# A hybrid DeltaNet and mLSTM trunk: the scheduler plays the program on its detailed machine model

## The chip, the cores and the metric

The kernel runs on one NeuronCore of a Trainium2 chip. The metric is the device time of one execution in microseconds (us). Five engines work side by side, each through its own fixed list of instructions: TensorE (PE; its weight loads are shown apart as PEld), VectorE (DVE), ScalarE (ACT), GpSimd (POOL) and SyncE (SP), which here only issues transfers. An engine goes through its list in order; an instruction whose input is not there yet holds up what stands behind it.

## What is computed

The reference is a trunk of two layers over 1040 tokens (16 learned ones and 1024 from the input) of width 1024. Each layer is a mixer and then a feed-forward block (FFN) with a causal convolution, each between two RMS norms. The first mixer is a gated DeltaNet with 16 value heads, the second an mLSTM with 4 heads. Cut to its core:

```python
for i in range(DEPTH):                      # DEPTH = 2
    a_in = rms_norm(hs, norm_w[i, 0])
    mix = gated_deltanet(a_in, ...) if i % 2 == 0 else mlstm(a_in, ...)
    hs = hs + keep * rms_norm(mix, norm_w[i, 1])
    f = conv_ffn(rms_norm(hs, norm_w[i, 2]), ...)
    hs = hs + keep * rms_norm(f, norm_w[i, 3])

# gated_deltanet, per head and chunk
a_mat = eye + einsum('id,jd->ij', kb, kc) * decay * strict
sol = triangular_solve(a_mat, rhs, lower=True)
v_new = u_c - w_c @ S
o_c = qd_c @ S + att_c @ v_new
S = S * gt_c + kt_c.T @ v_new

# conv_ffn
u = causal_depthwise_conv(h @ w_up, conv_w) + conv_b
return (silu(gate) * up) @ w_down
```

## The kernel before

Activations lie with the features on the 128 partitions and the tokens along the free axis. The DeltaNet and the mLSTM work on three blocks of 348 tokens, each of three chunks of 116; the FFN works on two halves of 520 tokens, each of two quarters of 260.

**Products.** A float32 product is made of three matmuls on split operands, high by high, high by low and low by high (`mm3`, lines 233 to 235). A weight is loaded raw by SyncE, its high part is made by ScalarE and its low part by GpSimd (`split_slot`):

```python
nc.scalar.copy(hi, part(raw))                                             # L137
nc.gpsimd.tensor_tensor(lo, part(raw), hi.bitcast(F32), ALU.subtract)     # L138
```

There are 9 slots for raw weights and 10 for split ones. A load into a raw slot waits until GpSimd has read the slot.

**Stages.** First the DeltaNet. Its work is cut into 24 steps, one for each pair of value heads and each block. In a step the function `weave` interleaves, in the program's text, the preparation of the next step (`gdn_prepare`), the recurrence of this one (`gdn_recur`), the finish of the last one and a share of the input projection (`gdn_project`, tiles named `pj_gi`). Near the end of the stage a first part of the output projection (`dn_go`) takes the place of the input projection. Then come the rest of the output projection with its norms, the FFN with its up projection (`up`; seven products per weight block in place of eight, whose partial sums VectorE adds at line 196) and its down projection (`dn_f`), the mLSTM, and the second FFN.

**The triangular inverse.** For each head `inverse` builds a masked matrix, starts the inverse from its 2 x 2 blocks and doubles the block size six times. VectorE writes the first `Z` at line 920, and three matmuls read it at once:

```python
nc.vector.tensor_tensor(Z, l0, Ib, ALU.add)                               # L920
px = bank("px", 0)
for c in range(NC_B):
    nc.tensor.matmul(px[:, c * CH : (c + 1) * CH], Z[:, c, :], I, ...)    # L923
nc.scalar.copy(f2(X), px[:, :BS])                                         # L924
```

Ahead of it VectorE makes `ah` (line 911) and `l0`. Each of the six levels then has three visits to TensorE (lines 949, 958 and 963) with a VectorE or ScalarE operation behind each; two more visits (lines 969 and 977) end it, and line 979 writes the result `XT`. Line 750 writes the normalised key at the beginning of `gdn_prepare`.

**The norms.** Squares are made by ScalarE (line 294) and added by VectorE (line 295); one matmul with a matrix of ones sums them over the partitions (line 302), and the call around it asks that it stay behind the matmul before it in the program:

```python
self.tc.keep_in_program_order(nc.tensor.matmul(ps, self.ones_f32, acc, ...))   # L302
```

The residual stream is updated at lines 352 and 353.

**What sets the order.** The kernel's text names the engine of every instruction, but it does not write the engines' lists. When the `TileContext` of line 1484 closes, a scheduler plays the whole program on a model of the machine. Whenever an engine of the model can take an instruction, it gets the one that is earliest in the program among those whose inputs and whose buffer slot are there in the model at that moment; a block under `high_priority(n)` counts as so many places earlier. The order in which the model took the instructions is the list of each engine on the chip, and the slot that a tile got there is its slot. The waits are put in afterwards. So a duration in the model moves an instruction in the list, and nothing moves any more once the program is compiled.

Of the kernel before, what the change touches and what calls it, by code (L numbers as in the profile page):

```python
# [1476 lines left out]
def build(nc, arrays):  # L1477
    from contextlib import ExitStack

    a = {}  # L1480
    for n, v in arrays.items():
        a[n] = nc.dram_tensor(f"in_{n}_dram", v.shape, mybir.dt.from_np(v.dtype), kind="ExternalInput").ap()
    a["out"] = nc.dram_tensor("out_0_dram", (D, SEQ), F32, kind="ExternalOutput").ap()
    with tile.TileContext(nc) as tc, ExitStack() as ctx:  # L1484
        Trunk(tc, a).run(ctx)


# [10 lines left out]
```

## Time and profile before

| quantity | value |
|---|---|
| runs shown, median (lowest to highest) | 3448.46 us (3437.92 to 3455.48), 3 runs |
| the profiled execution | 3444.23 us |
| its span, first to last instruction | 3442.5 us |
| mean granted TensorE clock | 0.969 |
| loaded and stored | 297.75 MB, 86 GB/s over the span |
| transfer engines busy, main queue | 26.3% |

Busy time and span are of the one profiled execution. A matmul's row lasts longer than the time until the next one can start, since matmuls overlap; so a busy TensorE is not TensorE at its peak, and the idle time, with what ended it, is what a change of order can act on. The stages by their lines: the DeltaNet runs until about 1160 us, its output projection until about 1300, the first FFN's up projection from about 1380 to 1830 and its down projection to about 2130, the mLSTM to about 2580, and the second FFN to the end.

### The profile page before, as it was taken

The page shows a single profiled execution, that of the slowest core. Times are in us where ns is not written, and L with a number is a line of the kernel's source. Part 1 is how long each engine was busy: PE and PEld are TensorE (multiplying, and loading weights), DVE is VectorE, ACT ScalarE, POOL GpSimd, SP SyncE. Part 2 cuts the span into 40 slices and gives each one's busy share as a digit, 9 for nine tenths or more (in the row PEclk, how much of TensorE's full clock was granted, in tenths as well). Part 3 has the DMA queues.
Part 4 walks back from the last instruction along what each step waited for, and adds up shares of the span by engine and source line. Part 5 has one row for each costly group of instructions (what it writes and reads, how often), then busy time and mean ns, then how long its engine had stood idle before and what let it go on. Part 6 is the DMA issues. An engine that isn't in the chain of part 4 may idle for free. (4 is left out here: it accounts for less than half of the span.)

```text
span 3442.5 us, 68429 instructions
## 1 busy us (share of the span) xinstructions
PE 3212.2 (93%) x25368; PEld 3119.6 (91%) x25368; DVE 2373.1 (69%) x5143; ACT 1609.0 (47%) x3390; POOL 1652.2 (48%) x1890
## 2 busy tenths in 40 slices
PE   7999999999999998799999989899998799999998
PEld 6889988988988897799999989899998799999998
DVE  7777777777767649877677484534469867777474
ACT  5455545555545435655455243323345645445232
POOL 2433443444334444577665434333344477666453
PEclk9999999999999999899999999999999899999999
DMA  3011100101001344422224453211125422224452
GB/s 118 23 37 34 34 29 31 34 32 34 31 31 40 107 132 152 134 93 93 78 78 133 133 182 125 93 44 50 56 78 183 136 90 87 87 75 132 132 180 88
DMA packets 234511, 297.75 MB, mean 86 GB/s; under 512 B 20684, under 2 KB 167104, under 8 KB 234176
## 3 DMA queue, kind: packets, MB, share of 16 engines
q1 hardware_dynamic: 234176, 293.37, 26.3%
q8 instruction: 200, 3.28, 0.4%
q14 instruction: 135, 1.11, 0.1%
HBM read 240.06 MB, written 53.23 MB: 85 GB/s over the span
## 5 line engine op out<-in xcount | busy, mean ns | idle before, releaser
L233 PE MATMUL pj_gi<-xh_in,wh_gi 128*128 128x348 f32 x1152 | 394.2, 342 | 5.5 <-ACT wh_gi L137 3.7
L233 PE MATMUL dn_f<-so_f,wh_f 128*128 128x260 f32 x1344 | 386.6, 288 | 11.8 <-ACT wh_f L137 5.0
L235 PE MATMUL pj_gi<-xh_in,wl_gi 128*128 128x348 f32 x1152 | 395.7, 343 | 0.9 <-POOL wl_gi L138 0.9
L234 PE MATMUL pj_gi<-xl_in,wh_gi 128*128 128x348 f32 x1152 | 393.5, 342 | 0.0
L235 PE MATMUL dn_f<-so_f,wl_f 128*128 128x260 f32 x1344 | 384.7, 286 | 0.0
L234 PE MATMUL dn_f<-so_f,wh_f 128*128 128x260 f32 x1344 | 384.5, 286 | 0.0
L138 POOL TENSOR_TENSOR wl_f<-wr_f,wh_f 128x512 fp32r<-128x512 f32 x168 | 226.0, 1362 | 246.0 <-ACT wh_f L137 113.5
L1278 DVE SCALAR_TENSOR_TENSOR z<-u,fcw,z 128x260 f32<-128x260 f32 x528 | 243.4, 487 | 49.8 <-ACT z L1276 35.0
L138 POOL TENSOR_TENSOR wl_u_s<-wr_u,wh_u_s 128x512 fp32r<-128x512 f32 x176 | 228.2, 1300 | 97.7 <-ACT wh_u_s L137 97.3
L233 PEld LDWEIGHTS dn_f<-so_f,wh_f 128*128 128x128 f32 x1344 | 257.7, 192 | 13.6 <-ACT z L1276 5.5
L441 DVE TENSOR_TENSOR acc_f<-acc_f,dn_f 128x260 f32<-128x260 f32 x320 | 133.1, 421 | 189.2 <-PE dn_f L235 188.2
L234 PEld LDWEIGHTS dn_f<-so_f,wh_f 128*128 128x128 f32 x1344 | 258.2, 192 | 0.2
L235 PEld LDWEIGHTS dn_f<-so_f,wl_f 128*128 128x128 f32 x1344 | 258.2, 192 | 0.1
L1276 ACT ACTIVATE z<-u,fcb,fcw 128x260 f32<-128x260 f32 x352 | 192.3, 570 | 93.7 <-DVE u L196 92.4
L233 PEld LDWEIGHTS pj_gi<-xh_in,wh_gi 128*128 128x128 f32 x1152 | 222.1, 193 | 8.0 <-ACT wh_gi L137 4.0
L235 PEld LDWEIGHTS pj_gi<-xh_in,wl_gi 128*128 128x128 f32 x1152 | 222.6, 193 | 2.4 <-POOL wl_gi L138 1.2
L234 PEld LDWEIGHTS pj_gi<-xl_in,wh_gi 128*128 128x128 f32 x1152 | 222.2, 193 | 0.7 <-issue 0.2
L138 POOL TENSOR_TENSOR wl_gi<-wr_gi,wh_gi 128x512 fp32r<-128x512 f32 x96 | 132.4, 1380 | 157.8 <-ACT wh_gi L137 153.8
L137 ACT CAST wh_u_s<-wr_u 128x512 fp32r<-128x512 f32 x176 | 105.9, 615 | 192.5 <-PE up L234 134.9
L697 DVE SCALAR_TENSOR_TENSOR gy<-u_g,c_gdn_conv_w_g,gy 128x348 f32<-128x348 f32 x288 | 187.9, 663 | 7.9 <-ACT gy L695 5.4
L138 POOL TENSOR_TENSOR wl_u_a<-wr_u,wh_u_a 128x512 fp32r<-128x512 f32 x132 | 170.1, 1293 | 37.0 <-ACT wh_u_a L137 36.3
L137 ACT CAST wh_f<-wr_f 128x512 fp32r<-128x512 f32 x168 | 103.1, 617 | 178.8 <-PE dn_f L234 133.0
(501 smaller groups left out, 11718.0 us busy)
## 6 DMA issues: line engine op xcount, KB each, us to landing
wr_u<-in_ffn_w_up_dram SPq DMA_DIRECT2D x224, 256.0 KB, 2.6
wr_f<-in_ffn_w_down_dram SPq DMA_DIRECT2D x176, 256.0 KB, 2.8
wr_gi<-in_gdn_w_in_dram SPq DMA_DIRECT2D x96, 256.0 KB, 2.6
h<-y SPq DMA_DIRECT2D x176, 130.0 KB, 2.3
si_f<-h SPq DMA_DIRECT2D x88, 260.0 KB, 3.5
wr_go<-in_gdn_w_out_dram SPq DMA_DIRECT2D x64, 256.0 KB, 2.7
wr_mi<-in_ml_w_in_dram SPq DMA_DIRECT2D x44, 256.0 KB, 2.6
o_g<-gy SPq DMA_DIRECT2D x48, 174.0 KB, 1.8
```

The lines of the kernel that those rows point to most:

```text
L137: nc.scalar.copy(hi, part(raw))
L138: nc.gpsimd.tensor_tensor(lo, part(raw), hi.bitcast(F32), ALU.subtract)
L233: nc.tensor.matmul(out, w[0], x[0], start=start, stop=False)
L234: nc.tensor.matmul(out, w[0], x[1], start=False, stop=False)
L235: nc.tensor.matmul(out, w[1], x[0], start=False, stop=stop)
L441: nc.vector.tensor_tensor(acc[m][n], acc[m][n], ps, ALU.add)
L697: ins = nc.vector.scalar_tensor_tensor(y, u[:, j : j + BS], taps[:, j : j + 1], y, ALU.mult, ALU.add)
L1276: nc.scalar.activation(z, p[:, 2 : 2 + QB], AF.Identity, scale=taps[:, 2:3], bias=self.fcb[:, tt : tt + 1])
L1278: nc.vector.scalar_tensor_tensor(z if i or not h else y[h], p[:, i : i + QB], taps[:, i : i + 1], z, ALU.mult, ALU.add)
```

## The change

The `TileContext` gets one argument. The scheduler then plays the program on the more detailed of its two machine models in place of the plain one. The kernel's text is otherwise the same: every instruction, its engine, its operands, the pools and the priorities.

```diff
     a["out"] = nc.dram_tensor("out_0_dram", (D, SEQ), F32, kind="ExternalOutput").ap()
-    with tile.TileContext(nc) as tc, ExitStack() as ctx:
+    with tile.TileContext(nc, schedule_with_timeline_sim=True) as tc, ExitStack() as ctx:
         Trunk(tc, a).run(ctx)
```

## The prediction

> **What bounds the kernel now.** The page comes first: the span, the busy times and the forty slices.
>
> ```profile
> span 3442.5 us, 68429 instructions
> ...
> PE 3212.2 (93%) x25368; PEld 3119.6 (91%) x25368; DVE 2373.1 (69%) x5143; ACT 1609.0 (47%) x3390; POOL 1652.2 (48%) x1890
> ...
> PE   7999999999999998799999989899998799999998
> ```
>
> TensorE (PE) is busy for 3212.2 of 3442.5 us, and nearly every slice is at nine tenths. So TensorE is the bound, and the whole idle time of the kernel's bound is 3442.5 - 3212.2 = 230.3 us. A change that adds and removes no instruction can win at most about that. The next view is the list of waits of TensorE alone: the line that waited, the line it waited for, total us, times, longest.
>
> ```profile
> PE px L923 <- DVE Z L920: 46.5, 40, 2.7
> PE up L233 <- DVE u L196: 21.5, 12, 1.8
> PE up L233 <- ACT u L1250: 17.4, 7, 6.8
> PE fs_f L302 <- DVE ss_f L295: 17.0, 4, 6.4
> PE fs_go L302 <- DVE ss_go L295: 16.2, 4, 5.3
> PE fs_mo L302 <- DVE ss_mo L295: 14.9, 4, 5.2
> PE S L848 <- DVE E L566: 10.0, 14, 0.9
> ...
> PE pj_gi L235 <- POOL wl_gi L138: 0.9, 1, 0.9
> ```
>
> What to see: TensorE waits for VectorE (DVE) above all, and hardly ever for GpSimd (POOL) or for a transfer. Three kinds make up half of the 230.3 us: the first matmul of the triangular inverse, which waits for Z (46.5 us, 40 times); the matmul that sums squares for a norm, which waits for the last addition (17.0 + 16.2 + 14.9 = 48.1 us, 12 times); and the up projection, which waits until its partial sums are read out (21.5 us, 12 times). Together 116.1 us. In all three an instruction stands at the head of TensorE's fixed order whose input is late, while matmuls that need nothing new stand behind it.
>
> Then the time by stage: us from the span's start, length, busy us (and count) of TensorE, its weight loads, VectorE, ScalarE and GpSimd, the granted clock, the DMA share and rate.
>
> ```profile
> 100.00:1160.00 1060.00, 991.33 (x8303) 943.78 (x8304) 790.48 (x1893) 536.61 (x1202) 419.05 (x507) 0.98 0.11 35
> ...
> 1290.00:1465.00 175.00, 140.73 (x1059) 136.82 (x1058) 155.36 (x288) 102.79 (x218) 85.65 (x91) 0.91 0.46 145
> ...
> 2580.00:2755.00 175.00, 143.34 (x1076) 139.21 (x1075) 159.22 (x296) 104.70 (x222) 83.30 (x90) 0.90 0.50 160
> ```
>
> The DeltaNet stage (100 to 1160 us) leaves TensorE 1060 - 991.3 = 68.7 us idle. The two passages from a mixer to its FFN (1290 to 1465, 2580 to 2755) leave 34.3 and 31.7 us, with VectorE at 89% and 91%, and the clock there is at 0.91 and 0.90.
>
> **The change part by part.** No instruction, operand or transfer is added or removed; only the model changes on which the scheduler plays the program. What can change is the order of each engine's instructions and which buffer a tile gets, so the sum has to be made of stalls.
>
> Why is an input late? One wait for Z, and what ran before it (start, us, engine, line, operation; the bracket is the idle time before); above it the spread of the two VectorE operations over the whole run (ns: min, median, max).
>
> ```profile
> L911 DVE TENSOR_TENSOR ah<-scs_kk,E x48: 504/774/1601, 92.1 to 1136.6; 116x348 f16<-116x348 f32 x48
> ```
>
> ```profile
> L920 DVE TENSOR_TENSOR Z<-l,i x48: 436/737/1393, 95.1 to 1139.1; 116x348 f16<-116x348 f16 x48
> ```
>
> ```profile
> 581.76 1.59 DVE L911 TENSOR_TENSOR ah<-scs_kk,E 116x348 f16<-116x348 f32 x1
> 583.28 1.07 DVE L920 TENSOR_TENSOR Z<-l,i 116x348 f16<-116x348 f16 x1
> ```
>
> ```profile
> 584.40 0.37 PE L923 MATMUL px<-i,Z 116*116 116x116 f16 x3 [1.38 <-DVE Z L920]
> ```
>
> The same operation on the same shape takes from 436 to 1393 ns. Here the two took (1.59 - 0.504) + (1.07 - 0.436) = 1.72 us more than at their shortest, and TensorE waited 1.38 us. What stretches VectorE shows in a passage:
>
> ```profile
> 1309.24 0.76 DVE L353 TENSOR_TENSOR hs_go<-hs_go,acc_go 128x260 f32<-128x260 f32 x2
> ...
> 1311.05 2.66 DVE L353 TENSOR_TENSOR hs_go<-hs_go,acc_go 128x260 f32<-128x260 f32 x2
> ```
>
> ```profile
> 1310.70 2.73 POOL L138 TENSOR_TENSOR wl_go<-wr_go,wh_go 128x512 fp32r<-128x512 f32 x2 [5.29 <-ACT wh_go L137]
> ```
>
> Two additions that take 0.76 us take 2.66 us while GpSimd subtracts. A model with one price for such an addition believes the norm's sum 1.9 us too early at this place alone, and puts the matmul that needs it too far forward. A model that prices the two engines together can put other matmuls ahead. That is what speaks for a gain.
>
> The terms. **Waits repaired**: bounds are 0 (the detailed model misses the same effect) and 116.1 us. I take half, 58 us: the stretch explains the first two kinds, but where two engines meet shifts by parts of a us, and no order fits every place. The rest of the idle time (230.3 - 116.1 = 114.2 us, the start, the tail and the chain behind the 17.4 us among it) I leave, since there ready work lacks rather than order. If the waits for Z go, the next late thing in that stage is S, which now waits 10.0 us in all.
>
> **The clock after a gap**: TensorE behind one norm matmul.
>
> ```profile
> 1319.70 1.24 PE L302 MATMUL fs_go<-ss_go,ones_f 128*128 128x260 f32 x2 [5.31 <-DVE ss_go L295]
> ...
> 1321.17 0.42 PE L233 MATMUL dn_go<-so_go,wh_go 128*128 128x260 f32 x1
> 1321.39 0.42 PE L234 MATMUL dn_go<-so_go,wh_go 128*128 128x260 f32 x1
> ...
> 1323.05 0.28 PE L234 MATMUL dn_go<-so_go,wh_go 128*128 128x260 f32 x1
> 1323.17 0.28 PE L235 MATMUL dn_go<-so_go,wl_go 128*128 128x260 f32 x1
> ```
>
> After 5.31 us without a matmul they start 0.22 us apart, and 0.12 us apart again some ten matmuls later: 10 x 0.10 = 1.0 us more per long gap. With half of the 12 norm waits gone, 6 x 1.0 = 6 us.
>
> **New waits**: a new order makes its own. Bounds: nothing, and a DeltaNet stage that fails as a whole (the first rival). I take the value nearest to a row: that the small waits of the DeltaNet stage come a second time. Its 68.7 us of idle time without its waits for Z,
>
> ```profile
> PE px L923 <- DVE Z L920: 45.6, 39, 2.7
> ```
>
> are 68.7 - 45.6 = 23 us more.
>
> **Transfers and slots**: every load and store is issued by SyncE (SP), whose order is played anew too.
>
> ```profile
> SPq L148 <- POOL wl_gi L138: 415.4, 81, 22.6
> ```
>
> The queue waits 415 us in all until GpSimd has freed a weight slot, and TensorE waited for such a weight only 0.9 us: weights stand ready ahead of need, and that cover hides a shifted load, so it costs nothing. Gone, each weight tile would come late by up to the wait above, 22.6 us at the longest.
>
> Sum: -58 - 6 + 23 = **-41 us**. The profiled execution took 3444.2 us, 1.7 more than its span, and lies 4 us under the median of the runs shown, 3448.5. So 3444 - 41 = **3403 us**. The case's own range: all 116.1 repaired and 12 us of clock with the 23 us of new waits gives 3339, a quarter repaired (-29 - 3 + 23) gives 3435.
>
> [...]
>
> **The rivals.** *First, slower: the chain of the DeltaNet stage is stretched.* If the detailed model lets an engine take work some way ahead of running it, an instruction that becomes ready lands behind work already placed. The place is the inverse, a chain that goes to TensorE and back about 24 times per (head, block) step: once for Z, three times in each of six levels, twice at the end, and three times before it. Its beginning and end, in the window 565 to 680 us, and two neighbouring projection matmuls:
>
> ```profile
> L750 DVE TENSOR_TENSOR gy<-gy,rs_k x3: 501/509/522, 571.8 to 665.4; 128x348 f32<-128x348 f32 x3
> ```
>
> ```profile
> L979 DVE SCALAR_TENSOR_TENSOR XT<-Z,px_f x4: 507/508/518, 608.3 to 656.6; 116x348 f32<-116x348 f16 x4
> ```
>
> ```profile
> 580.11 0.32 PE L234 MATMUL pj_gi<-xl_in,wh_gi 128*128 128x348 f32 x1
> 580.27 0.32 PE L235 MATMUL pj_gi<-xh_in,wl_gi 128*128 128x348 f32 x1
> ```
>
> A step recurs every (665.4 - 571.8) / 2 = 46.8 us, and the chain from key to inverse takes 608.3 - 571.8 = 36.5. The slack is 10.3 us, or 10.3 / 24 = 0.43 us per visit, 2.7 projection matmuls of 0.16 us. That is the point from which it decides: with 2.7 more of them ahead of each visit the stage is as long as now, and with four it is 24 x 1.3 x 0.16 = 5.0 us longer per step, 24 steps, **+120 us, 3564**. For it: the stage is the longest and its order is now fine-grained. Against it: filler is bounded by buffers, so such runs end soon.
>
> [...]
>
> *Second, no difference*: position in the program and the hand-set priorities decide most picks on a saturated engine, so the order hardly moves, or the waits only change places. Then the change does not do what it says for the chip: **3444**. For it: 93% busy. Against it: the 40 waits for Z are picks that a price decides.
>
> *Third, all three kinds vanish and none is new*: -116 - 12 = -128, **3316**.
>
> **How the numbers follow.** Forecast 0.41, first rival 0.36, second 0.17, third 0.06. The first rival stays near the forecast because its chain passes TensorE so often with so little slack. A measurement of this kernel tells about 0.5% (17 us) from no change. Of the forecast's 0.41, 0.02 lie within that, so faster is 0.39 + 0.06 = 0.45, same 0.17 + 0.02 = 0.19, slower 0.36. The range runs from 3330, just under the forecast's low end, to 3570, just over the first rival's price; outside lie most of the third rival and the worse part of the first, under 0.2.
>
> **What would show it.** Right: the waits of L923 for Z and of the norm matmuls at about half, the DeltaNet stage some 20 us shorter, the clock in the passages above 0.91. The first rival: the recurrence of L979 over 47 us and longer runs of projection matmuls between the inverse's small ones. The second: the same waits at other places. Wrong altogether, in either direction, if TensorE's idle time moves in the FFN stages, or if its weights or transfers come late, for none of which I have a term.

## The result and the profile after

| | before | after |
|---|---|---|
| time, median (lowest to highest) | 3449.32 us (3437.92 to 3455.48), 4 runs | 3527.45 us (3527.17 to 3530.81), 4 runs |
| ratio after to before, 95% interval | | 1.0233 (1.0205 to 1.026) |
| profiled execution | 3444.23 us | 3527.17 us |
| its span | 3442.5 us | 3525.2 us |
| mean granted TensorE clock | 0.969 | 0.943 |

The change makes the kernel 2.3% slower, 83 us in the profiled executions; 3403 us, 41 us faster, was forecast. The page after, with the slices of the granted clock:

```profile
span 3525.2 us, 68243 instructions
...
PE 3290.2 (93%) x25368; PEld 3196.9 (91%) x25368; DVE 2384.7 (68%) x5143; ACT 1613.0 (46%) x3408; POOL 1659.3 (47%) x1890
...
PE   8989899898889899989999999999999799999998
...
PEclk9889889898989899989999999999999899999999
```

The same slices of the clock, before:

```profile
PEclk9999999999999999899999999999999899999999
```

TensorE is busy for the same 93%, with the same 25368 matmuls. Whoever reads only the share of busy time sees nothing. But its busy time grew by 78 us, and the row of the clock shows where: in the first 14 slices (the DeltaNet stage) many now stand at 8 where all stood at 9.

Where the 83 us arose is seen by cutting both executions at the same place, the first matmul of the first FFN's up projection that reads a weight `wh_u_a`: the DeltaNet, its output projection and the first 576 matmuls of the up projection lie ahead of it, everything else behind it. Before (us from the start, length, busy us and count of TensorE, its weight loads, VectorE, ScalarE and GpSimd, clock, DMA share, GB/s):

```profile
0.00:1460.90 1460.90, 1335.68 (x10851) 1271.95 (x10852) 1091.20 (x2491) 743.94 (x1633) 588.55 (x684) 0.97 0.19 61
1460.90:3442.50 1981.60, 1876.52 (x14519) 1847.66 (x14517) 1281.89 (x2653) 865.10 (x1757) 1063.61 (x1207) 0.97 0.33 105
```

After:

```profile
0.00:1592.90 1592.90, 1433.42 (x10852) 1365.72 (x10853) 1077.79 (x2484) 744.06 (x1645) 586.77 (x681) 0.90 0.17 56
1592.90:3525.20 1932.30, 1856.77 (x14519) 1831.16 (x14517) 1306.89 (x2660) 868.94 (x1764) 1072.53 (x1210) 0.98 0.34 108
```

The same matmuls stand on either side of the cut (one may be counted on both). The first part takes 132.0 us more, the second 49.3 us less: a loss and a gain at different places. Of the loss, 1433.4 - 1335.7 = 97.7 us are longer busy time at a lower clock (0.90 for 0.97) and 159.5 - 125.2 = 34.3 us are idle time. The gain is 29.6 us of idle time and 19.8 us of busy time.

The list of TensorE's waits after has the gain in it:

```profile
PE px L923 <- DVE Z L920: 21.2, 23, 1.7
PE ks L828 <- DVE St L854: 14.3, 16, 2.0
PE up L233 <- ACT u L1250: 11.4, 6, 4.5
PE px L963 <- DVE X L959: 9.0, 16, 0.9
...
PE fs_mo L302 <- DVE ss_mo L295: 8.2, 3, 6.9
...
PE fs_go L302 <- DVE ss_go L295: 6.1, 2, 5.9
...
PE fs_f L302 <- DVE ss_f L295: 4.6, 3, 2.3
...
PE up L233 <- DVE u L196: 0.2, 1, 0.2
```

The waits for Z went from 46.5 to 21.2 us, the three norms from 48.1 to 18.9, the wait for the partial sums from 21.5 to 0.2. Other waits are new or longer (`ks` for St, 14.3 us). Over the whole run TensorE is idle for 3525.2 - 3290.2 = 235.0 us, before for 230.3: of the 82.7 us by which the span grew, 78.0 are busy time. So most of the loss is not in this list; in it, others wait for TensorE. In the waits of all engines, before:

```profile
ACT Z L964 <- PE px L963: 115.8, 128, 2.3
...
DVE X L959 <- PE px L958: 29.8, 74, 0.8
```

After:

```profile
ACT Z L964 <- PE px L963: 246.0, 96, 8.4
...
DVE X L959 <- PE px L958: 120.0, 95, 3.4
```

These are two of the three answers in a level of the triangular inverse. ScalarE waits 2.6 us on average for its matmul (246.0 / 96) in place of 0.9. What it waits behind is seen in the timeline after (start, us, engine, line). VectorE first:

```profile
628.30 0.87 DVE L920 TENSOR_TENSOR Z<-l,i 116x348 f16<-116x348 f16 x1
```

TensorE in the same microseconds:

```profile
627.36 0.49 PE L234 MATMUL pj_gi<-xl_in,wh_gi 128*128 128x348 f32 x1
627.65 0.49 PE L235 MATMUL pj_gi<-xh_in,wl_gi 128*128 128x348 f32 x1
...
629.19 0.32 PE L235 MATMUL pj_gi<-xh_in,wl_gi 128*128 128x348 f32 x1
629.35 0.32 PE L233 MATMUL pj_gi<-xh_in,wh_gi 128*128 128x348 f32 x1
...
631.57 0.32 PE L235 MATMUL pj_gi<-xh_in,wl_gi 128*128 128x348 f32 x1
631.73 0.32 PE L923 MATMUL px<-i,Z 116*116 116x116 f16 x3
```

Z is there at 628.30 + 0.87 = 629.17. Its matmul runs at 631.73, after 16 projection matmuls that need nothing from the inverse (629.19 to 631.57, 0.16 us apart). Two things are to be seen. The wait of TensorE for Z is gone here, and a wait of the chain for TensorE has taken its place. And the projection matmuls at 627.36 follow each other at 0.29 us, those at 629.35 at 0.16, so the rate changed in between.

The step's recurrence by line 750, before and after:

```profile
L750 DVE TENSOR_TENSOR gy<-gy,rs_k x24: 501/514/671, 85.3 to 1122.4; 128x348 f32<-128x348 f32 x24
```

```profile
L750 DVE TENSOR_TENSOR gy<-gy,rs_k x24: 499/506/1315, 97.3 to 1297.0; 128x348 f32<-128x348 f32 x24
```

(1122.4 - 85.3) / 23 = 45.1 us became (1297.0 - 97.3) / 23 = 52.2 us.

### The profile page after: what moved, and what is told of

Its sections match the earlier page's. It is cut to its first block, busy times and chain, and to the rows that moved or that the text cites. A ratio compares the mean times of both kernels' runs of the same rounds, so it can differ in the third digit from the quotient of the medians.

```text
span 3525.2 us, 68243 instructions
## 1 busy us (share of the span) xinstructions
PE 3290.2 (93%) x25368; PEld 3196.9 (91%) x25368; DVE 2384.7 (68%) x5143; ACT 1613.0 (46%) x3408; POOL 1659.3 (47%) x1890
## 5 line engine op out<-in xcount | busy, mean ns | idle before, releaser
L233 PE MATMUL pj_gi<-xh_in,wh_gi 128*128 128x348 f32 x1152 | 400.4, 348 | 12.0 <-DVE u_g L308 6.8
L233 PE MATMUL dn_f<-so_f,wh_f 128*128 128x260 f32 x1344 | 385.6, 287 | 15.0 <-DVE acc_f L439 5.0
L233 PEld LDWEIGHTS dn_f<-so_f,wh_f 128*128 128x128 f32 x1344 | 255.7, 190 | 18.0 <-ACT z L1276 7.1
L233 PEld LDWEIGHTS pj_gi<-xh_in,wh_gi 128*128 128x128 f32 x1152 | 230.7, 200 | 17.2 <-DVE u_g L308 9.1
L234 PEld LDWEIGHTS pj_gi<-xl_in,wh_gi 128*128 128x128 f32 x1152 | 229.9, 200 | 0.5
L964 ACT CAST Z<-px 116x168 f16<-116x168 f32 (+4 forms) x288 | 88.5, 328 | 256.7 <-PE px L963 246.0
L697 DVE SCALAR_TENSOR_TENSOR gy<-u_g,c_gdn_conv_w_g,gy 128x348 f32<-128x348 f32 x288 | 178.7, 633 | 28.7 <-ACT gy L695 26.8
L138 POOL TENSOR_TENSOR wl_u_a<-wr_u,wh_u_a 128x512 fp32r<-128x512 f32 x132 | 175.4, 1338 | 18.3 <-ACT wh_u_a L137 17.1
```

The lines of the kernel that those rows point to most:

```text
L233: nc.tensor.matmul(out, w[0], x[0], start=start, stop=False)
L234: nc.tensor.matmul(out, w[0], x[1], start=False, stop=False)
L697: ins = nc.vector.scalar_tensor_tensor(y, u[:, j : j + BS], taps[:, j : j + 1], y, ALU.mult, ALU.add)
L964: nc.scalar.copy(od(Z), fo(zo, NC_B))
```

## The experiments

The theory: the detailed model has a queue for each engine, into which the model's sequencer puts instructions ahead of running them (35 for TensorE, 12 for each other engine). What is taken keeps its place, so a visit of the inverse that becomes ready a little later lands behind projection matmuls that were taken when nothing else was ready. The queue belongs to the scheduler's model; only the order reaches the chip. The rivals: the detailed durations (*prices*) give the worse order, whatever the queues (the price theory); the order of the picks (*rank*) does, and a priority would mend it; and the loss is not the delay but the *clock* that falls in the bare stretches (the stage got 0.97 before and 0.88 after).

A count goes with the times: the matmuls of the input and output projection that stand, in TensorE's list, between the first visit of an inverse (L923) and its last (L977), the mean of the 48 inverses. An inverse has 21 such visits, so 20 gaps lie between them. The count is **51 before and 137 after**: 86 / 20 = 4.3 more per visit. From the first inverse to the last, the longest run of them is 78 matmuls before and 24 after, but the 78 stand between two inverses. Of the gaps between the visits of one inverse, only 5% hold 12 or more before, and 30% after.

In the experiments "stage" is the start of the last input projection matmul (`pj_gi`, L233), 1113.1 us before and 1243.1 us after. All runs but the last two leave the program's instructions as they are. A queue is set around the changed `TileContext`:

```diff
+    from concourse.hw_specs import TRN2Spec
...
+    kept = TRN2Spec.ENG_ISSUE_QUEUE_DEPTH
+    TRN2Spec.ENG_ISSUE_QUEUE_DEPTH = {e: 2 for e in kept}
     with tile.TileContext(nc, schedule_with_timeline_sim=True) as tc, ExitStack() as ctx:
         Trunk(tc, a).run(ctx)
+    TRN2Spec.ENG_ISSUE_QUEUE_DEPTH = kept
```

All results in one table; the texts follow. The ratio, with its interval, is to executions of the kernel before that were timed beside the run (their medians lie between 3443.64 and 3449.32 us), so runs are best compared by it.

| run | queue of TensorE / others | projection matmuls per inverse | stage, us | time, us | ratio |
|---|---|---|---|---|---|
| before | plain model | 51 | 1113.1 | 3449.32 | 1 |
| after | 35 / 12 | 137 | 1243.1 | 3527.45 | 1.0233 (1.0205 to 1.026) |
| e1 | 2 / 2 | 57 | 1078.5 | 3352.62 | 0.9729 (0.9715 to 0.9744) |
| e2 | 2 / 12 | 54 | 1112.5 | 3390.58 | 0.9838 (0.9823 to 0.9853) |
| e3 | 35 / 2 | 134 | 1241.2 | 3528.75 | 1.0237 (1.0218 to 1.0257) |
| e4 | 4 / 4 | 64 | 1069.8 | 3354.68 | 0.9731 (0.9717 to 0.9746) |
| e5 | 35 / 12, priority | 137 | 1244.7 | 3531.61 | 1.0236 (1.0219 to 1.0254) |
| e6 | 12 / 4 | 95 | 1027.9 | 3313.32 | 0.9602 (0.9587 to 0.9618) |
| e7 | 24 / 4 | 118 | 1168.4 | 3452.33 | 1.0006 (0.9988 to 1.0024) |
| e8 | 4 / 4, priority | 59 | 1070.0 | 3350.32 | 0.9712 (0.9693 to 0.9732) |
| e9 | 12 / 12 | 95 | 1038.2 | 3317.15 | 0.9632 (0.9615 to 0.9648) |
| e10 | 8 / 4 | 89 | 1052.8 | 3332.95 | 0.968 (0.9666 to 0.9695) |
| e11 | 35 / 12, 576 matmuls added | 133 | 1224.8 | 3520.77 | 1.0225 (1.021 to 1.024) |
| e12 | 35 / 12, 1152 matmuls added | 130 | 1269.6 | 3566.44 | 1.0361 (1.0346 to 1.0377) |

### Is it the queue, and whose?

e1 cuts every queue to 2 (the diff above):

> The detailed model, but each engine of the model may hold only 2 instructions that it has taken and not finished. In its compiled order an inverse has on average 57 projection matmuls between its first and last visit to TensorE, against 51 in the kernel before and 137 in the changed one. Queue theory (the model's long queue lets TensorE take projection matmuls ahead of an inverse's next step): the last matmul of the input projection, now at 1243 us and before at 1113, comes at 1113 within 15 us, the waits for Z and the clock of the DeltaNet stage are near those of before, the later stages keep the 47 us that they won, and the time is about 3400 us, 3380 to 3430. [...]

e2 cuts TensorE's alone:

```diff
+    TRN2Spec.ENG_ISSUE_QUEUE_DEPTH = {e: 2 if e == mybir.EngineType.PE else 12 for e in kept}
```

> Only TensorE's queue in the model is cut to 2, the others keep the detailed model's 12. Per inverse 54 projection matmuls in the compiled order. Queue theory, with TensorE's queue as the cause: as with all queues cut, 3380 to 3430 us. If the queues of VectorE and ScalarE are what delays the chain: between, 3460 to 3530 us. Price theory: 3500 to 3530 us.

e3 cuts all but TensorE's:

```diff
+    TRN2Spec.ENG_ISSUE_QUEUE_DEPTH = {e: 35 if e == mybir.EngineType.PE else 2 for e in kept}
```

> The complement: TensorE's queue keeps its 35, all others are cut to 2. Per inverse 134 projection matmuls in the compiled order. Queue theory with TensorE's queue as the cause: no repair, 3500 to 3535 us, the DeltaNet stage at a clock under 0.90. If the other queues are the cause: 3400 to 3450 us. Price theory: 3500 to 3530 us, so this run does not part it from the first.

e4 sets all to 4:

```diff
+    TRN2Spec.ENG_ISSUE_QUEUE_DEPTH = {e: 4 for e in kept}
```

> All queues of the model cut to 4: 64 projection matmuls per inverse. Queue theory: near the run with 2, up to 15 us longer in the DeltaNet stage for its longer chain, or shorter if the finer mixing keeps TensorE fuller (the bare stretches without a projection matmul are shorter in its order, 13.9 against 15.3 matmuls, weighted); 3380 to 3440 us. Price theory: 3500 to 3530 us.

The windows up to the end of the stage, e2 and then e3:

```profile
0.00:1112.50 1112.50, 1028.74 (x8435) 975.07 (x8436) 857.02 (x1991) 585.50 (x1292) 434.38 (x534) 0.98 0.12 38
```

```profile
0.00:1241.20 1241.20, 1113.86 (x8175) 1053.62 (x8176) 805.88 (x1918) 548.69 (x1239) 421.81 (x522) 0.88 0.11 34
```

With TensorE's queue at 2 the loss is gone, stage and clock are back; with the others at 2 and TensorE's at 35 it is all there, and the count is 134. So it is TensorE's queue. The prices are the detailed ones in all four, and the kernel is 2.7% faster than before in e1 and e4: the price rival falls. Both came out better than expected, 27 and 25 us under the 3380 us at which their ranges began, and the stage of e1 ended 34.6 us ahead of the kernel before: a short queue does more than take the loss away. With the short queue of TensorE, long queues of the others cost too (e2 is 38 us above e1); with one of 12 hardly (0.9632 in e9, 0.9602 in e6).

### Is it the rank?

e5 lets the preparation of the next step, which holds the inverse, count as 3000 places earlier; e8 does the same with all queues at 4:

```diff
-                parts.insert(0, (self.gdn_prepare(n + 1, tb, lb), 27))
+                parts.insert(0, (self.rush(self.gdn_prepare(n + 1, tb, lb)), 27))
...
+    def rush(self, g):
+        while True:
+            with self.tc.high_priority(3000):
+                try:
+                    next(g)
+                except StopIteration:
+                    return
+            yield
```

> The detailed model with its own queues, and every instruction of the preparation of a DeltaNet step under a priority of 3000 places. In the compiled order an inverse still has 137 projection matmuls in it, as in the changed kernel; under the plain model the same priority lowers 51 to 36. Queue theory (the projection matmuls are taken before the inverse's next instruction is ready, so rank can't help): no repair, 3505 to 3540 us, the input projection ending at 1243 us within 20. Rank theory (the detailed durations let the projection outrank the chain): 3380 to 3450 us.

> All queues 4 and the preparation under the priority of 3000. The chain is then offered and can be taken soon: 59 projection matmuls per inverse against 64 without the priority. Queue theory: the chain has slack already, so little: 3335 to 3365 us. A fall below 3335 would say that the chain still bounds the stage with queues of 4.

In e5 the count stays at 137 and the ratio at 1.0236 for 1.0233. That is what the queue theory says: a priority decides among instructions that are ready, and the projection matmuls were taken before the visit was ready. e8 can't be told from e4 (the intervals overlap). The rank theory falls.

### How much per matmul, and from where?

e6, e7, e9 and e10 set TensorE's queue to 12, 24, 12 and 8, the others' to 4, 4, 12 and 4:

```diff
+    TRN2Spec.ENG_ISSUE_QUEUE_DEPTH = {e: 12 if e == mybir.EngineType.PE else 4 for e in kept}
```

> TensorE's queue in the model 12, the others 4: 95 projection matmuls per inverse in the compiled order, 2.2 more per visit than in the kernel before (51), under the 2.7 at which the prediction's first rival begins to cost. Queue theory with that threshold: the input projection ends as with all queues at 4 (1070 us), within 15, and the time is 3350 to 3375 us. If every added matmul costs from the first one on (no slack): 64 to 95 is a third of the way to the changed kernel's 137 and its 1243 us, so about 1140 us and 3420 us.

> TensorE's queue 24, the others 4: 118 per inverse, 3.35 more per visit than before. With the threshold of 2.7: 0.65 matmuls of 0.16 us over 24 visits and 24 steps, 60 us more than the run with all queues at 4, the projection's end at 1130 us and the time at about 3415. Without a threshold, in proportion: 1070 + 173 x (118 - 64) / (137 - 64) = 1198 us and about 3480.

> TensorE's queue in the model 12, all others at the detailed model's own 12. Per inverse 95 projection matmuls in the compiled order. If TensorE's queue is what matters and 12 is short enough: within 1% of the run with TensorE at 12 and the others at 4 (3313 us), so 3305 to 3350. If the other queues hold back the same chain as in the run with only TensorE cut to 2 (3391 against 3353 with all cut): about 3345 to 3360.

> TensorE 8, the others 4: 89 projection matmuls per inverse, longest run of projection matmuls 27, against 95 and 16 with TensorE at 12 and 64 and 68 with TensorE at 4. If evenness (no long run of projection matmuls, no long stretch without) gives the gain of the run with 12: between 3313 and 3355, nearer the first, 3315 to 3335. If what counts is only that the chain stays under its slack: as with 4, 3345 to 3360.

The stage falls from 1078.5 to 1027.9 us as TensorE's queue goes from 2 over 4 and 8 to 12, then rises to 1168.4 at 24 and 1243.1 at 35. In projection matmuls per visit beyond the kernel before ((count - 51) / 20): 0.3, 0.65, 1.9, 2.2, then 3.35 and 4.3. So up to 2.2 more cost nothing, and 3.35 do; the point of 2.7 that the prediction worked out from the slack lies between. A cost in proportion to the count falls by e6 alone, which it put at 1140 us. e7 does not decide: its 1168.4 us lie between the 1130 with the point and the 1198 in proportion, nearer the second, so past the point the price was too small.

But the slack is not the reason. The prediction took it as the step less the chain from key to inverse, 46.8 - 36.5 us. Two keys of e6 (line 750), in the window 590 to 640 us, and then the two inverses that belong to the first of them (line 979, one for each head), in the window 601 to 640:

```profile
L750 DVE TENSOR_TENSOR gy<-gy,rs_k x2: 506/510/515, 595.1 to 634.4; 128x348 f32<-128x348 f32 x2
```

```profile
L979 DVE SCALAR_TENSOR_TENSOR XT<-Z,px_f x2: 517/517/517, 636.8 to 639.9; 116x348 f32<-116x348 f16 x2
```

The step takes 634.4 - 595.1 = 39.3 us, and the two heads' inverses come 41.7 and 44.8 us after their key, when the next key is already written. The later of the two inverses comes after the next key in all 23 pairs of steps, in e6 and in the changed kernel alike. Preparations of two steps can overlap, so a chain longer than a step costs nothing by itself. That the point of 2.7 fits the runs is luck; where between 2.2 and 3.35 the cost begins, and why there, stays open.

That e6 would be better still than e4 was not expected: its time is 37 us and its stage 27 us under the ranges of the queue theory. Its page:

```profile
span 3310.2 us, 68157 instructions
...
PE 3168.3 (96%) x25368; PEld 3090.6 (93%) x25368; DVE 2393.4 (72%) x5143; ACT 1600.7 (48%) x3393; POOL 1654.2 (50%) x1890
...
PEclk9999999999999998999999999999998899999999
```

Its part ahead of the first FFN and the rest, cut as above:

```profile
1384.70:3310.20 1925.50, 1853.41 (x14519) 1829.07 (x14517) 1302.05 (x2658) 862.33 (x1757) 1071.01 (x1207) 0.98 0.35 109
...
0.00:1384.70 1384.70, 1314.92 (x10851) 1261.52 (x10852) 1091.31 (x2486) 738.33 (x1636) 583.23 (x684) 0.98 0.20 64
```

Against before, 76.2 us are won ahead of the cut and 56.1 behind it. Behind it e6 and the changed kernel are 7 us apart (1925.5 and 1932.3), and all runs with the detailed model lie between 1925 and 1940 us there, for 1981.6 before. So the gain of the detailed model there hardly hangs on the queue; nearly all that the queue decides is ahead of the cut. In the order of e6 the projection matmuls stand in short, even runs: no run is over 16, against 78 before and 68 in e4. That more even filler is the reason for e6's lead fits e10, which lies between in longest run (27) and time, but no run changed the evenness alone.

### Is it the clock?

e11 puts one more matmul, whose result nobody uses, ahead of two of the three visits in each level of the inverse; e12 puts two:

```diff
             pp = bank("pp", s)
             pv = fe(pp[:, : NC_B * ne], NC_B)
+            for _ in range(1):
+                nc.tensor.matmul(pp[:, :BS], ah[:, 0, :], f2(ah), start=True, stop=True)
...
             px = bank("px", s)
+            for _ in range(1):
+                nc.tensor.matmul(px[:, :BS], ah[:, 0, :], f2(ah), start=True, stop=True)
```

> The changed kernel with one more matmul (fp16, 116 rows, 348 columns) ahead of the first and of the second visit of every level, into the bank that the visit then overwrites: 576 matmuls, at some 0.15 us about 85 us of TensorE work whose result is not used, issued while the chain waits. Clock theory (the half-speed clock in the stretches without projection matmuls is a price of its own: 0.88 in the stage against 0.97 before): the clock of the stage rises and its end does not come later in spite of the added work, 1200 to 1245 us, total 3480 to 3530. Symptom theory (the chain's waits alone set the pace): the clock rises or not, the end moves from 1243 to 1260 or later, total 3540 to 3615.

> The same with two such matmuls at each place, about 170 us of added work. Clock theory: the clock of the stage near 1.0; the added work no longer fits the idle time, 3500 to 3600 us. Symptom theory: later by up to the added work, 3600 to 3700 us.

The stage in the changed kernel, in e11 and in e12:

```profile
0.00:1243.10 1243.10, 1111.70 (x8176) 1050.85 (x8177) 802.44 (x1918) 556.36 (x1249) 420.20 (x522) 0.88 0.10 34
```

```profile
0.00:1224.80 1224.80, 1132.95 (x8699) 1054.66 (x8700) 811.26 (x1921) 562.91 (x1253) 420.50 (x522) 0.94 0.11 35
```

```profile
0.00:1269.60 1269.60, 1187.23 (x9223) 1107.12 (x9224) 819.07 (x1921) 565.20 (x1252) 428.33 (x522) 0.96 0.11 34
```

With 8699 - 8176 = 523 more matmuls the stage ends 18.3 us *earlier*. At the 0.16 us at which matmuls of 348 columns follow each other above, the added ones are an estimated 84 us of work; the others then keep TensorE busy for 1133 - 84 = 1049 us in place of 1112, at a clock of 0.94 for 0.88. In e12 the clock rises to 0.96, but 1047 matmuls more no longer fit, and the stage ends 26.5 us later. The added matmuls also move the order a little, to 133 and 130 projection matmuls per inverse for 137; but e3, with 134, has the whole loss (1241.2 us, 0.88), so that does not shorten the stage. So the clock has a price of its own, an estimated 60 us of busy time in e11, and work that nobody needs can lower it; the delay of the chain stays, and as a remedy this is worth 0.2% at most (3520.77 for 3527.45 us; the interval of e11 overlaps that of the change).

## Why the prediction was wrong

**The repair came, larger than forecast.** The three kinds of wait took 116.1 us and now take 21.2 + 18.9 + 0.2 = 40.3: 75.8 us are repaired, where half, 58, was taken. Ahead of the cut, where Z and `fs_go` stand, they are 25.3 + 10.1 = 35.4 us; behind it 12.4 + 6.7 + 21.3 = 40.4, where the time fell by 49.3. The reason given also held in part. VectorE still gets stretched before Z, in the median more than before:

```profile
L920 DVE TENSOR_TENSOR Z<-l,i x48: 322/874/1056, 110.9 to 1317.2; 116x348 f16<-116x348 f16 x48
```

The median is 874 ns for 737, yet TensorE waits for Z half as much (21.2 us for 46.5). That the waits only change places, as the second rival has it, was borne out ahead of the cut, where idle time grew by 34.3 us, though in other waits than those repaired, and not behind it, where it fell by 29.6. That idle time moved in the FFN stages was named as a sign of being wrong altogether, but the up projection's 21.3 us among it were a term of the sum.

**The clock after a gap** was taken as -6 us, with the clock in the passages above 0.91. The two passages, each the 175 us around the start of an FFN as before:

```profile
1422.00:1597.00 175.00, 150.89 (x1148) 146.88 (x1147) 163.83 (x299) 109.68 (x231) 90.81 (x94) 0.93 0.46 146
2679.50:2854.50 175.00, 145.49 (x1067) 140.22 (x1066) 160.03 (x294) 107.27 (x224) 82.18 (x89) 0.90 0.51 161
```

0.91 and 0.90 became 0.93 and 0.90. The term was too small to show, and of the wrong sign for the kernel: the clock that counted was the DeltaNet's, and it fell from 0.97 to 0.88 in the stage.

**The step that failed is "New waits".** It was +23 us, "that the small waits of the DeltaNet stage come a second time". Measured, the part ahead of the cut lost 132.0 us although 35.4 us of waits were repaired there: 167 us of new cost, seven times the term. Under it lies a premise that failed too, that "the sum has to be made of stalls": 97.7 of the 132.0 us are TensorE's busy time, at a clock of 0.90 for 0.97.

The other bound of this term was named in the same place, the first rival, and it is what happened, with its mechanism (work taken some way ahead), its place (the inverse) and its mark (more runs of projection matmuls between the visits; a recurrence over 47 us, now 52.2 by line 750). Its size also came near: "with four it is ... +120 us", and 4.3 more per visit were found. That is luck in part, since the sum rests on the slack, which e6 contradicts, and leaves out the clock. The time of 3564 was too high since the rival was priced alone: the forecast and the rival were treated as cases that exclude each other. Most of each stands in another stage, and both came: 3444 - 49 + 132 = 3527.

**Why the rival was given 0.36 and not more.** The reason against it was that "filler is bounded by buffers, so such runs end soon". A count of the runs would have questioned it, since before the change one run, between two inverses, already had 78 matmuls. What decided was TensorE's queue in the model, 35 long: the ratio is 1.0233 with it and 0.9632 with one of 12 (e9).

**What the rival's sum left out** is the clock: it was 24 visits by 1.3 matmuls, all delay. In the changed kernel the stretches without projection matmuls are long, and the clock falls in them: counted in the trace, pauses of over 5 us from one projection matmul to the next make up 390 us of the stage, 5 before, and 227 of the stage's 300 us at half clock lie in them. (A row of one is at the end.) How much of the 130 us by which the stage grew is the clock has an upper estimate, from its lengths and the missing share of the clock (0.12 after, 0.03 before): 1243.1 x 0.12 - 1113.1 x 0.03 = 116 us.

**The other rivals.** "No difference" falls with the interval. That all waits vanish at no cost (3316) did not happen here, but e6 comes to 3313 us by the same detailed prices, close to it by chance, with 8.9 + 11.2 + 7.7 + 7.2 = 35.0 us left of the waits for Z and the three norms, 94.6 before:

```profile
PE fs_f L302 <- DVE ss_f L295: 11.2, 3, 6.6
PE px L923 <- DVE Z L920: 8.9, 12, 2.2
PE fs_go L302 <- DVE ss_go L295: 7.7, 3, 5.0
PE fs_mo L302 <- DVE ss_mo L295: 7.2, 2, 5.1
```

**Left open.** Which of the detailed model's prices brings the gain (that of two engines beside each other, of a matmul, of a transfer) was not separated. Why a queue of 12 beats 4 is argued from the order, not shown; and how the 132 us divide between the delay of the chain and the clock is known from e11 only roughly, since added matmuls also delay the chain. What bounds a step of the changed kernel at 52.2 us, now that the slack does not, was not found.

## What to carry to other kernels

When TensorE is saturated and a long chain returns to it many times, count the independent matmuls that an order puts ahead of each visit, and look at the clock in the stretches left without them (here 0.50 from 680 to 690 us). A scheduler that commits an engine's order ahead of readiness decides this count, and here a priority of 3000 places took nothing back. A slack worked out as step less chain bounds nothing where the steps can overlap. A better machine model and a deep queue in it are two changes: try them apart (here 1.0233 with a queue of 35, 0.9602 with one of 12). And before a rival is set against a forecast, ask whether they act in different stages: then both can come, and their sums add.

## What was not expected of the hardware

An order alone changed the granted clock. The stage, up to its last input projection matmul, before and in e6:

```profile
0.00:1113.10 1113.10, 1033.71 (x8434) 977.50 (x8435) 839.62 (x1990) 571.96 (x1278) 431.81 (x533) 0.97 0.12 38
```

```profile
0.00:1027.90 1027.90, 996.08 (x8245) 950.94 (x8246) 819.98 (x1935) 551.83 (x1246) 416.65 (x522) 0.99 0.13 41
```

Some 8200 to 8400 matmuls got 0.97 before and 0.99 in e6, with TensorE busy for 93% and 97% of the stage; after, at 89%, the clock was 0.88. In ten-microsecond windows of the changed kernel:

```profile
600.00:610.00 10.00, 10.00 (x93) 9.85 (x93) 5.78 (x14) 3.38 (x9) 2.98 (x5) 1.00 0.17 54
...
680.00:690.00 10.00, 9.37 (x57) 8.87 (x55) 8.03 (x22) 6.41 (x15) 1.99 (x3) 0.50 0.06 19
```

From 680 to 690 us TensorE is busy for 94% of the time, at half the clock. The counts of 93 and 57 matmuls are not of one kind: 35 of the first are projection matmuls and none of the second. But the same line shows the rate, in the first window and in the second:

```profile
600.45 0.30 PE L958 MATMUL px<-pl,Z 116*116 116x64 f16 x3
600.59 0.40 PE L274 MATMUL kn<-ah_k,ones 128*128 128x348 f32 x1
```

```profile
684.59 0.45 PE L958 MATMUL px<-pl,Z 116*116 116x56 f16 x3
684.86 0.48 PE L963 MATMUL px<-i,X 116*116 116x58 f16 x3
```

Three matmuls of 64 columns make way after 0.14 us, three of 56 columns after 0.27. So the rows show two rates, at a clock of 1.00 and of 0.50. What the chip grants them by no run here shows; it is not the busy share of the profile alone, since 94% had 0.50 from 680 to 690 us and 93% had 0.97 in the stage before. And work that nobody uses made the stage 18.3 us shorter (e11), with a clock of 0.94 for 0.88.
